# Row kurtosis on one core: 16 equal groups of 64 rows, loads in pieces, and an order written by hand

## The chip, the cores and the metric

The kernel runs on one core of a Trainium2 chip. The metric is the time of one execution in microseconds (us) on the device; lower is better. Engines are named as the profile names them: PE (matmul and transpose), DVE (vector), ACT (scalar activations), POOL (GpSimd) and SP (which issues loads). Each engine has its own queue of instructions and works it off in order; engines wait for one another through semaphores.

## The reference

The input `x` is 1024 rows of 8192 float32 values (33.55 MB). For each row the reference computes the excess kurtosis:

```python
mean = np.mean(x, axis=-1, keepdims=True)
std = np.std(x, axis=-1, keepdims=True)
z = (x - mean) / (std + 1e-8)
return (np.mean(z ** 4, axis=-1) - 3).astype(np.float32)
```

A kernel needs three sums for each row: the sum of the values, the sum of the squared differences from the mean, and the sum of their fourth powers. The result is N times the third divided by the square of the second, minus 3.

## The kernel before, in words

The rows are cut into 24 groups. `PLAN` gives a number k for each: a group has 128/k rows, and each row is spread over k partitions with 8192/k values in each. So k = 2 means 64 rows, a tile of 128 partitions by 4096 values, 2 MB. The plan begins with two groups of k = 8 and one of k = 4, has thirteen of k = 2, and ends with two of k = 4, two of k = 8 and four of k = 16. Each group is one load (L188, on SP's queue) into a slot of the `xpool`; there are 10 slots for the groups of k = 2.

For each group these steps follow:

- The mean. For k = 2 (the function `mean`, L116): PE transposes the 32 blocks of 128 columns and lets them add up in one PSUM tile `tps` (L123, "the turn" in what follows); DVE adds the two partitions of a row and writes the sum to both places, `red` (L129); PE multiplies `red` with a column of -1/8192, `negcol`, which gives minus the mean for each partition, `mps` (L134); ACT copies it to `nmu` (L137). For the other k (`mean_dve`, L92): DVE adds the halves of the tile with a running sum (L96), PE adds up the partitions of a row with the block matrix `blk[k]` (L103), ACT copies (L105).
- The square (L192): ACT writes (x - mean) squared over the tile and its row sums into a column of `sa`.
- The fourth power of the group before (`fourth`, L165): DVE multiplies the tile with itself and writes the sum into `sd` (L175). Each fifth group has it on ACT instead (L171), into a column of `sa`; the last group is halved between the two.
- When a batch of neighbouring groups with the same k is through, `finish_batch` (L145): PE adds the partitions of a row for the squares (`p2`, L151) and for the fourth powers (`p4`, L152 and L153), DVE forms the result (L155 to L160), and a DMA writes it out (L163). There are six batches.

The Python loop gives the order in which the work is stated. The order on each engine is then made by the framework's scheduler, which goes by its own model of durations, and semaphores are set by it too. POOL builds the block matrices (L52 to L57) for each k, clears `sa` and `sd` (L85, L86), and then makes the identity matrix `ident` (L109, L110) that the transposes need, and `negcol` (L114).

Of the kernel before, what the change touches and what calls it, by code (L numbers as in the profile page):

```python
# [7 lines left out]
f32 = mybir.dt.float32  # L8
bf16 = mybir.dt.bfloat16
AO = mybir.AluOpType  # L10
AF = mybir.ActivationFunctionType
P = 128


PLAN = [8, 8, 4, 2, 2, 2, 2, 2, 2, 2, 2, 2, 2, 2, 2, 2, 4, 4, 8, 8, 16, 16, 16, 16]
SLOTS = {2: 10, 4: 2, 8: 2, 16: 4}


@with_exitstack
def kernel(  # L20
    ctx: ExitStack,
    tc: tile.TileContext,
    x: bass.AP,
    out: bass.AP,
):
    nc = tc.nc
    n_rows, n_cols = x.shape
    neg_inv_n = -1.0 / float(n_cols)
    assert sum(P // k for k in PLAN) == n_rows

    xpool = ctx.enter_context(tc.tile_pool(name="xpool", bufs=1))
    const = ctx.enter_context(tc.tile_pool(name="const", bufs=1))
    junkp = ctx.enter_context(tc.tile_pool(name="junkp", bufs=1))
    small = ctx.enter_context(tc.tile_pool(name="small", bufs=6))
    fin = ctx.enter_context(tc.tile_pool(name="fin", bufs=2))
    psum = ctx.enter_context(tc.tile_pool(name="psum", bufs=2, space=bass.MemoryType.PSUM))
    psfin = ctx.enter_context(tc.tile_pool(name="psfin", bufs=1, space=bass.MemoryType.PSUM))


    warm = const.tile([P, 1], f32, name="warm")  # L40
    nc.vector.memset(warm, 0.0)
    nc.scalar.activation(out=warm, in_=warm, func=AF.Square)


    blk = {}

    def block_matrix(k):
        if k not in blk:
            r = P // k
            b = const.tile([P, P], f32, name=f"blk{k}")  # L50
            v = b.rearrange("p (r k) -> p r k", k=k)
            nc.gpsimd.memset(b, neg_inv_n)  # L52
            nc.gpsimd.affine_select(  # L53
                out=v, in_=v, pattern=[[-k, r], [0, k]], base=0,
                channel_multiplier=1, compare_op=AO.is_ge, fill=0.0,
            )
            nc.gpsimd.affine_select(  # L57
                out=v, in_=v, pattern=[[k, r], [0, k]], base=k - 1,
                channel_multiplier=-1, compare_op=AO.is_ge, fill=0.0,
            )  # L60
            blk[k] = b
        return blk[k]

    for k in PLAN:
        block_matrix(k)

    groups = []
    row = 0
    for k in PLAN:
        groups.append((row, k, P // k, n_cols // k))  # L70
        row += P // k


    batches = []
    for i, g in enumerate(groups):
        if batches and groups[batches[-1][0]][1] == g[1] and len(batches[-1]) < 64:
            batches[-1].append(i)
        else:
            batches.append([i])
    where = {}  # L80
    for b in batches:
        n = len(b)
        sa = const.tile([P, 2 * n], f32, name=f"sa{b[0]}")
        sd = const.tile([P, n], f32, name=f"sd{b[0]}")
        nc.gpsimd.memset(sa, 0.0)  # L85
        nc.gpsimd.memset(sd, 0.0)  # L86
        for j, i in enumerate(b):
            where[i] = (b, j, n, sa, sd)

    junk = junkp.tile([P, 1024], bf16, name="junk")  # L90

    def mean_dve(i, xt):  # L92
        row, k, r, w = groups[i]
        h = w // 2
        part = small.tile([P, 1], f32, name="part")
        nc.vector.tensor_tensor_reduce(  # L96
            out=junk[:, :h], in0=xt[:, :h], in1=xt[:, h:],
            scale=neg_inv_n if k == 1 else 1.0, scalar=0.0,
            op0=AO.add, op1=AO.add, accum_out=part)
        if k == 1:  # L100
            return part
        mps = psum.tile([P, 1], f32, name="mps")
        nc.tensor.matmul(mps, lhsT=blk[k], rhs=part, start=True, stop=True)  # L103
        nmu = small.tile([P, 1], f32, name="nmu")
        nc.scalar.copy(nmu, mps)  # L105
        return nmu

    ident = const.tile([P, P], f32, name="ident")
    nc.gpsimd.memset(ident, 1.0)  # L109
    nc.gpsimd.affine_select(  # L110
        out=ident, in_=ident, pattern=[[-1, P]], base=0,
        channel_multiplier=1, compare_op=AO.is_equal, fill=0.0)
    negcol = const.tile([P, 1], f32, name="negcol")
    nc.gpsimd.memset(negcol, neg_inv_n)  # L114

    def mean(i, xt):  # L116
        row, k, r, w = groups[i]
        if k > 2:
            return mean_dve(i, xt)
        ch = w // P  # L120
        tps = psum.tile([P, P], f32, name="tps")
        for c in range(ch):
            nc.tensor.matmul(tps, lhsT=xt[:, c * P:(c + 1) * P], rhs=ident,  # L123
                             start=c == 0, stop=c == ch - 1, is_transpose=True)
        red = small.tile([P, P], f32, name="red")
        if k == 1:
            nc.vector.tensor_copy(red, tps)
        else:
            nc.vector.tensor_reduce(  # L129
                out=red.rearrange("p (r k) -> p r k", k=k),  # L130
                in_=tps.rearrange("p (r k) -> p r k", k=k).unsqueeze(2).to_broadcast([P, r, k, k]),
                op=AO.add, axis=mybir.AxisListType.X)
        mps = psum.tile([P, 1], f32, name="mps")
        nc.tensor.matmul(mps, lhsT=red, rhs=negcol,  # L134
                         start=True, stop=True)
        nmu = small.tile([P, 1], f32, name="nmu")
        nc.scalar.copy(nmu, mps)  # L137
        return nmu

    def split(i, w):  # L140
        if i == len(groups) - 1:
            return w // 2
        return w if i % 5 == 2 else 0

    def finish_batch(b):  # L145
        _, _, n, sa, sd = where[b[0]]
        row, k, r, w = groups[b[0]]
        sel = blk[k].rearrange("p (r k) -> p r k", k=k)[:, :, 0]
        p2 = psfin.tile([n, r], f32, name="p2")
        p4 = psfin.tile([n, r], f32, name="p4")  # L150
        nc.tensor.matmul(p2, lhsT=sa[:, 0:n], rhs=sel, start=True, stop=True)  # L151
        nc.tensor.matmul(p4, lhsT=sa[:, n:2 * n], rhs=sel, start=True, stop=False)  # L152
        nc.tensor.matmul(p4, lhsT=sd, rhs=sel, start=False, stop=True)  # L153
        rec = fin.tile([n, r], f32, name="rec")
        nc.vector.reciprocal(rec, p2)  # L155
        kr = fin.tile([n, r], f32, name="kr")
        nc.vector.scalar_tensor_tensor(  # L157
            out=kr, in0=p4, scalar=-1.0, in1=rec, op0=AO.mult, op1=AO.mult)
        nc.vector.tensor_mul(kr, kr, rec)  # L159
        nc.vector.tensor_scalar_add(kr, kr, -3.0)  # L160
        dst = out[row:row + n * r].rearrange("(g r) -> g r", r=r)
        eng = nc.sync if b is batches[-1] else nc.scalar
        eng.dma_start(out=dst, in_=kr)  # L163

    def fourth(i):  # L165
        row, k, r, w = groups[i]
        b, j, n, sa, sd = where[i]
        xt = tiles[i]
        cl = split(i, w)
        if cl > 0:  # L170
            nc.scalar.activation(  # L171
                out=xt[:, :cl], in_=xt[:, :cl], func=AF.Square,
                accum_out=sa[:, n + j:n + j + 1])
        if cl < w:
            nc.vector.tensor_tensor_reduce(  # L175
                out=xt[:, cl:], in0=xt[:, cl:], in1=xt[:, cl:], scale=1.0, scalar=0.0,
                op0=AO.mult, op1=AO.add, accum_out=sd[:, j:j + 1])
        if j == n - 1:
            finish_batch(b)

    tiles = {}
    used = {}
    for i, (row, k, r, w) in enumerate(groups):
        s = used.get(w, 0)
        used[w] = s + 1
        xt = xpool.tile([P, w], f32, name=f"x{k}", tag=f"x{k}_{s % SLOTS[k]}")
        tiles[i] = xt
        nc.sync.dma_start(  # L188
            out=xt, in_=x[row:row + r, :].rearrange("r (k w) -> (r k) w", k=k))
        nmu = mean(i, xt)  # L190
        b, j, n, sa, sd = where[i]
        nc.scalar.activation(  # L192
            out=xt, in_=xt, func=AF.Square, bias=nmu, accum_out=sa[:, j:j + 1])
        if i > 0:
            fourth(i - 1)
    fourth(len(groups) - 1)


# [28 lines left out]
```

## Time and profile before

| | us |
|---|---|
| median of 3 runs | 134.70 |
| lowest and highest run | 134.06, 134.92 |
| the profiled execution | 134.22 |
| its span, first to last instruction | 132.5 |
| busy: ACT | 80.2 |
| busy: PE | 74.8 |
| busy: DVE | 73.6 |
| busy: POOL | 5.8 |

The mean granted clock of PE was 0.802. The loads moved 33.56 MB in 24 transfers. A profile line of a group of instructions reads: line, engine, operation, output <- input, shapes, count, busy time and mean duration, idle time of the engine just before, and what ended that idle time. In the slices, the span is cut into 40 equal parts of 3.3 us, and each digit is the busy share in tenths.

### The profile page before, as it was taken

The numbers are of one execution on the slowest core, as the hardware profiler recorded it, in microseconds if no ns is written. First come the engines' busy times: TensorE is split into PE (matmuls) and PEld (weight loads), VectorE is DVE, ScalarE is ACT, GpSimd is POOL, SyncE is SP. The second block draws the span as 40 slices with busy tenths as digits, with TensorE's granted clock in tenths as the row PEclk, the third lists the DMA queues.
The fourth block names the chain that finished last, engine by engine and source line by source line (L and its number), as shares of the span: only waits on it lengthen the run. The fifth ranks groups of instructions, "written<-read, shape, count | busy, mean of one in ns | idle before, by whom it ended". The sixth has DMA issues, their size and how long they took to land. (4 is left out here: it accounts for less than half of the span.)

```text
span 132.5 us, 1379 instructions
## 1 busy us (share of the span) xinstructions
PE 74.8 (56%) x500; PEld 69.0 (52%) x500; DVE 73.6 (56%) x98; ACT 80.2 (61%) x86; POOL 5.8 (4%) x31
## 2 busy tenths in 40 slices
PE   0223999419894298789403989168999202115430
PEld 0221989319794297779303979067989101014420
DVE  0458011580299709610996069931015999998881
ACT  4076608309292196999901948047899694449890
POOL 8900000000000000000000000000000000000000
PEclk9999999985699959999995599965589975555555
DMA  4999999999999999999999996000000000000000
GB/s 114 433 462 415 420 445 401 425 435 401 465 406 450 415 435 435 401 460 406 455 406 406 419 403 232 0 2 0 0 0 7 0 0 0 0 0 1 0 0 0
DMA packets 3511, 33.64 MB, mean 254 GB/s; under 512 B 433, under 2 KB 433, under 8 KB 1457
## 3 DMA queue, kind: packets, MB, share of 16 engines
q1 hardware_dynamic: 3464, 33.56, 60.5%
q8 instruction: 4, 0.07, 0.2%
q14 instruction: 3, 0.02, 0.0%
q10 hardware_dynamic: 40, 0.00, 0.0%
HBM read 33.55 MB, written 0.00 MB: 253 GB/s over the span
## 5 line engine op out<-in xcount | busy, mean ns | idle before, releaser
L175 DVE CUSTOM_DVE_ANT_0 x<-x 128x4096 f32<-128x4096 f32 (+4 forms) x19 | 57.4, 3027 | 10.1 <-ACT x L192 5.0
L192 ACT ACTIVATE x<-x,nmu 128x4096 f32<-128x4096 f32 (+3 forms) x24 | 61.7, 2573 | 1.3 <-DVE kr L160 0.6
L123 PE MATMUL tps<-ident,x 128*128 128x128 f32 x416 | 61.2, 318 | 0.3 <-DMA x<-in_x_dram 0.3
L123 PEld LDWEIGHTS tps<-ident,x 128*128 128x128 f32 x416 | 59.6, 172 | 0.4 <-issue 0.4
L129 DVE TENSOR_REDUCE red<-tps 128x128 f32<-128x256 f32 x13 | 5.5, 423 | 38.2 <-PE tps L123 38.2
L137 ACT COPY nmu<-mps 128x1 f32<-128x1 f32 x13 | 2.0, 155 | 36.0 <-PE mps L134 36.0
L134 PE MATMUL mps<-negcol,red 128*128 128x1 f32 x26 | 5.5, 282 | 27.4 <-DVE red L129 27.4
L134 PEld LDWEIGHTS mps<-negcol,red 128*128 128x128 f32 x26 | 4.7, 225 | 30.5 <-issue 19.1
L171 ACT ACTIVATE x<-x 128x2048 f32<-128x2048 f32 (+3 forms) x6 | 12.1, 2013 | 0.9 <-DVE rec L155 0.8
L103 PE MATMUL mps<-part,blk 128*128 128x1 f32 x22 | 6.1, 358 | 10.5 <-DVE part L96 10.5
L103 PEld LDWEIGHTS mps<-part,blk 128*128 128x128 f32 x22 | 5.4, 315 | 11.6 <-issue 7.7
L96 DVE CUSTOM_DVE_ANT_0 junk<-x 128x512 bf16<-128x512 f32 (+2 forms) x11 | 8.1, 737 | 5.7 <-DMA x<-in_x_dram 5.7
L105 ACT COPY nmu<-mps 128x1 f32<-128x1 f32 x11 | 1.4, 153 | 10.4 <-PE mps L103 10.4
L151 PE MATMUL p<-blk,sa 128*2 128x16 f32 (+4 forms) x12 | 1.6, 218 | 10.4 <-ACT x L192 8.7
L151 PEld LDWEIGHTS p<-blk,sa 128*2 128x2 f32 (+3 forms) x12 | 0.6, 85 | 11.0 <-ACT x L192 9.1
L153 PE MATMUL p<-blk,sd 128*2 128x16 f32 (+4 forms) x12 | 1.6, 222 | 5.4 <-DVE sd L175 5.3
L192 ACT ACTIVATION_READ_ACCUMULATOR x<-x,nmu 128x1 f32 x24 | 4.5, 187 | 0.0
L153 PEld LDWEIGHTS p<-blk,sd 128*2 128x2 f32 (+3 forms) x12 | 0.8, 92 | 5.7 <-DVE sd L175 4.0
L57 POOL TENSOR_SCALAR_AFFINE_SELECT blk<-blk 128x128 f32<-128x128 f32 x4 | 2.1, 545 | 0.0
L155 DVE RECIPROCAL rec<-p 2x16 f32<-2x16 f32 (+4 forms) x6 | 1.9, 317 | 0.3 <-PE p L151 0.2
L152 PE MATMUL p<-blk,sa 128*2 128x16 f32 (+4 forms) x12 | 1.5, 206 | 1.0 <-ACT x L171 0.8
L53 POOL TENSOR_SCALAR_AFFINE_SELECT blk<-blk 128x128 f32<-128x128 f32 x4 | 1.9, 501 | 0.0
(20 smaller groups left out, 11.5 us busy)
## 6 DMA issues: line engine op xcount, KB each, us to landing
x<-in_x_dram SPq DMA_DIRECT2D x13, 2048.0 KB, 27.9
x<-in_x_dram SPq DMA_DIRECT2D x3, 1024.0 KB
x<-in_x_dram SPq DMA_DIRECT2D x4, 512.0 KB, 3.9
x<-in_x_dram SPq DMA_DIRECT2D x4, 256.0 KB, 14.4
out_dram<-kr ACTq DMA_DIRECT2D x3, 0.1 KB
out_dram<-kr ACTq DMA_DIRECT2D x1, 3.2 KB
out_dram<-kr ACTq DMA_DIRECT2D x1, 0.2 KB
out_dram<-kr SPq DMA_DIRECT2D x1, 0.1 KB
```

The lines of the kernel that those rows point to most:

```text
L57: nc.gpsimd.affine_select(out=v, in_=v, pattern=[[k, r], [0, k]], base=k - 1, channel_multiplier=-1, compare_op=AO.is_ge, fill=0.0,)
L96: nc.vector.tensor_tensor_reduce(out=junk[:, :h], in0=xt[:, :h], in1=xt[:, h:], scale=neg_inv_n if k == 1 else 1.0, scalar=0.0, op0=AO.add ...
L103: nc.tensor.matmul(mps, lhsT=blk[k], rhs=part, start=True, stop=True)
L123: nc.tensor.matmul(tps, lhsT=xt[:, c * P:(c + 1) * P], rhs=ident, start=c == 0, stop=c == ch - 1, is_transpose=True)
L129: nc.vector.tensor_reduce(out=red.rearrange("p (r k) -> p r k", k=k), in_=tps.rearrange("p (r k) -> p r k", k=k).unsqueeze(2).to_broadcast ...
L134: nc.tensor.matmul(mps, lhsT=red, rhs=negcol, start=True, stop=True)
L137: nc.scalar.copy(nmu, mps)
L151: nc.tensor.matmul(p2, lhsT=sa[:, 0:n], rhs=sel, start=True, stop=True)
L153: nc.tensor.matmul(p4, lhsT=sd, rhs=sel, start=False, stop=True)
L171: nc.scalar.activation(out=xt[:, :cl], in_=xt[:, :cl], func=AF.Square, accum_out=sa[:, n + j:n + j + 1])
L175: nc.vector.tensor_tensor_reduce(out=xt[:, cl:], in0=xt[:, cl:], in1=xt[:, cl:], scale=1.0, scalar=0.0, op0=AO.mult, op1=AO.add, accum_out ...
L192: nc.scalar.activation(out=xt, in_=xt, func=AF.Square, bias=nmu, accum_out=sa[:, j:j + 1])
```

## The change

All 1024 rows go in 16 equal groups of 64 rows (k = 2), so that the mean is always taken by transposes; `mean_dve` and the block matrices are gone, and a matrix `sel` of 128 by 64 takes the place of the block matrices in the finish. Each group is loaded in four pieces of 1024 columns (512 KB each), and there are 12 slots of whole tiles. `tc.manual_schedule()` makes the order on each engine the order in which the program states it: all loads first on SP; on PE the turn, then the mean; on DVE the reduce of group i, then the fourth power of group i-1; on ACT the copy, the square, and then the fourth power of the first 512 columns of the same group. DVE takes the other 3584 columns. In the last group ACT takes 2304 columns and DVE 1792. The groups form three batches (12, 3 and 1); the finish is divided in `second_moment` and `finish`, and all outputs are issued on SP. `sa` and `sd` are no longer cleared, as all of their columns are written.

```diff
-PLAN = [8, 8, 4, 2, 2, 2, 2, 2, 2, 2, 2, 2, 2, 2, 2, 2, 4, 4, 8, 8, 16, 16, 16, 16]
-SLOTS = {2: 10, 4: 2, 8: 2, 16: 4}
+K = 2
+GROUPS = 16
+CHUNK = 1024
+SLOTS = 12
+ACT_S4 = 512
+LAST_ACT_S4 = 2304
+LAG_BATCH = 12
...
+    R = P // K
+    W = n_cols // K
+    xpool = ctx.enter_context(tc.tile_pool(name="xpool", bufs=SLOTS))
...
+    ctx.enter_context(tc.manual_schedule())
...
+    batches = [list(range(LAG_BATCH)), list(range(LAG_BATCH, GROUPS - 1)), [GROUPS - 1]]
...
+    def load(i):
+        xt = xpool.tile([P, W], f32, name="xt")
+        xts[i] = xt
+        src = x[i * R:(i + 1) * R, :].rearrange("r (k w) -> (r k) w", k=K)
+        for c in range(0, W, CHUNK):
+            nc.sync.dma_start(out=xt[:, c:c + CHUNK], in_=src[:, c:c + CHUNK])
+
+    def turn(i):
         tps = psum.tile([P, P], f32, name="tps")
+        tpss[i] = tps
+        for c in range(0, W, P):
+            nc.tensor.matmul(tps, lhsT=xts[i][:, c:c + P], rhs=ident,
+                             start=c == 0, stop=c == W - P, is_transpose=True)
+
+    def reduce(i):
         red = small.tile([P, P], f32, name="red")
+        nc.vector.tensor_reduce(
+            out=red.rearrange("p (r k) -> p r k", k=K),
+            in_=tpss[i].rearrange("p (r k) -> p r k", k=K).unsqueeze(2).to_broadcast([P, R, K, K]),
+            op=AO.add, axis=AX)
+
+    def mean(i):
         mps = psum.tile([P, 1], f32, name="mps")
+        nc.tensor.matmul(mps, lhsT=reds[i], rhs=negcol, start=True, stop=True)
         nmu = small.tile([P, 1], f32, name="nmu")
         nc.scalar.copy(nmu, mps)
+        mpss[i] = nmu
+
+    def square(i):
+        j, n, sa, sd = where[i]
+        nc.scalar.activation(out=xts[i], in_=xts[i], func=AF.Square, bias=mpss[i],
+                             accum_out=sa[:, j:j + 1])
+
+    def fourth_act(i, c):
+        j, n, sa, sd = where[i]
+        nc.scalar.activation(out=xts[i][:, :c], in_=xts[i][:, :c], func=AF.Square,
+                             accum_out=sa[:, n + j:n + j + 1])
+
+    def fourth_dve(i, c):
+        j, n, sa, sd = where[i]
+        nc.vector.tensor_tensor_reduce(
+            out=xts[i][:, c:], in0=xts[i][:, c:], in1=xts[i][:, c:], scale=1.0, scalar=0.0,
+            op0=AO.mult, op1=AO.add, accum_out=sd[:, j:j + 1])
+
+    def second_moment(b):
+        j, n, sa, sd = where[b[0]]
+        p2 = psfin.tile([n, R], f32, name="p2")
         nc.tensor.matmul(p2, lhsT=sa[:, 0:n], rhs=sel, start=True, stop=True)
+        rec = fin.tile([n, R], f32, name="rec")
+        nc.vector.reciprocal(rec, p2)
+        rec2 = fin.tile([n, R], f32, name="rec2")
+        nc.vector.scalar_tensor_tensor(
+            out=rec2, in0=rec, scalar=-1.0, in1=rec, op0=AO.mult, op1=AO.mult)
+        return rec2
+
+    def finish(b, rec2):
+        j, n, sa, sd = where[b[0]]
+        p4 = psfin.tile([n, R], f32, name="p4")
         nc.tensor.matmul(p4, lhsT=sa[:, n:2 * n], rhs=sel, start=True, stop=False)
         nc.tensor.matmul(p4, lhsT=sd, rhs=sel, start=False, stop=True)
+        kr = fin.tile([n, R], f32, name="kr")
+        nc.vector.tensor_mul(kr, p4, rec2)
         nc.vector.tensor_scalar_add(kr, kr, -3.0)
+        dst = out[b[0] * R:(b[0] + n) * R].rearrange("(g r) -> g r", r=R)
+        nc.sync.dma_start(out=dst, in_=kr)
+
+    L = GROUPS - 1
+    for i in range(GROUPS):
+        load(i)
+    for i in range(GROUPS):
+        turn(i)
+        reduce(i)
+        mean(i)
+        square(i)
+        if i >= 1:
+            fourth_dve(i - 1, ACT_S4)
+        if i < L:
+            fourth_act(i, ACT_S4)
+        if i == LAG_BATCH + 1:
+            finish(batches[0], second_moment(batches[0]))
+    rec2 = second_moment(batches[1])
+    rec2l = second_moment(batches[2])
+    fourth_act(L, LAST_ACT_S4)
+    fourth_dve(L, LAST_ACT_S4)
+    finish(batches[1], rec2)
+    finish(batches[2], rec2l)
```

The pools `psum` (two buffers each of `tps` and `mps`) and `psfin` (one buffer each of `p2` and `p4`) are as before.

More of the change, by code (lines that the diff above doesn't have):

```diff
@@ L42 @@
     nc.scalar.activation(out=warm, in_=warm, func=AF.Square)
[L45 to L106, printed above, removed]
     ident = const.tile([P, P], f32, name="ident")
@@ L114 @@
     nc.gpsimd.memset(negcol, neg_inv_n)
[L116 to L120, printed above, removed]
-        tps = psum.tile([P, P], f32, name="tps")
-        for c in range(ch):
-            nc.tensor.matmul(tps, lhsT=xt[:, c * P:(c + 1) * P], rhs=ident,
-                             start=c == 0, stop=c == ch - 1, is_transpose=True)
-        red = small.tile([P, P], f32, name="red")
[L126 to L132, printed above, removed]
+    sel = const.tile([P, R], f32, name="sel")
@@ new lines @@
+    nc.gpsimd.memset(sel, neg_inv_n)
+    nc.gpsimd.affine_select(
+        out=sel, in_=sel, pattern=[[-K, R]], base=0,
+        channel_multiplier=1, compare_op=AO.is_ge, fill=0.0)
+    nc.gpsimd.affine_select(
+        out=sel, in_=sel, pattern=[[K, R]], base=K - 1,
+        channel_multiplier=-1, compare_op=AO.is_ge, fill=0.0)
+    one = const.tile([1, 1], f32, name="one")
+    nc.gpsimd.memset(one, 1.0)
+    batches = [list(range(LAG_BATCH)), list(range(LAG_BATCH, GROUPS - 1)), [GROUPS - 1]]
@@ new lines @@
+    where = {}
+    for b in batches:
+        n = len(b)
+        sa = const.tile([P, 2 * n], f32, name=f"sa{b[0]}")
+        sd = const.tile([P, n], f32, name=f"sd{b[0]}")
+        for j, i in enumerate(b):
+            where[i] = (j, n, sa, sd)
+    xts = {}
+    tpss = {}
+    reds = {}
+    mpss = {}
+    def load(i):
[4 more added lines that the diff above has]
+            nc.sync.dma_start(out=xt[:, c:c + CHUNK], in_=src[:, c:c + CHUNK])
@@ L133, in mean @@
+    def mean(i):
         mps = psum.tile([P, 1], f32, name="mps")
-        nc.tensor.matmul(mps, lhsT=red, rhs=negcol,
-                         start=True, stop=True)
+        nc.tensor.matmul(mps, lhsT=reds[i], rhs=negcol, start=True, stop=True)
         nmu = small.tile([P, 1], f32, name="nmu")
         nc.scalar.copy(nmu, mps)
[L138 to L151, printed above, removed]
+        mpss[i] = nmu
@@ L152, in finish_batch @@
         nc.tensor.matmul(p4, lhsT=sa[:, n:2 * n], rhs=sel, start=True, stop=False)
         nc.tensor.matmul(p4, lhsT=sd, rhs=sel, start=False, stop=True)
[L154 to L195, printed above, removed]
@@ L196 @@
-    fourth(len(groups) - 1)
+        kr = fin.tile([n, R], f32, name="kr")
+        nc.vector.tensor_mul(kr, p4, rec2)
+        nc.vector.tensor_scalar_add(kr, kr, -3.0)
+        dst = out[b[0] * R:(b[0] + n) * R].rearrange("(g r) -> g r", r=R)
[14 more added lines that the diff above has]
+            finish(batches[0], second_moment(batches[0]))
```

10 lines of the change are left out of this document (5 added, 5 removed).

## The prediction

> **What bounds the kernel now.** I read the page first (engine totals, then the 40 slices), then the waits, then the timeline at two places.
>
> ```profile
> span 132.5 us, 1379 instructions
> PE 74.8 (56%) x500; PEld 69.0 (52%) x500; DVE 73.6 (56%) x98; ACT 80.2 (61%) x86; POOL 5.8 (4%) x31
> DVE  0458011580299709610996069931015999998881
> ACT  4076608309292196999901948047899694449890
> DMA  4999999999999999999999996000000000000000
> ```
>
> No engine is busy for more than 61% of the span. The DMA engines are full from slice 1 to slice 23 and stop in slice 24, at about 82 us; for the last 50 us no input moves, and DVE and ACT work off what is left. So the end is set by compute that fell behind the loads. Nor is that compute short of throughput: while the loads ran, DVE and ACT had many slices of 0 to 3. The waits say why.
>
> ```profile
> DVE red L129 <- PE tps L123: 38.2, 7, 6.3
> ACT nmu L137 <- PE mps L134: 36.0, 10, 6.0
> PE mps L134 <- DVE red L129: 27.4, 13, 7.5
> ```
>
> The columns are total us, times, longest. Three engines wait in a ring for one another. The timeline shows one turn of it, then a stretch where the order happens to be right:
>
> ```profile
> 24.56 4.43 DVE L175 CUSTOM_DVE_ANT_0 x<-x 128x4096 f32<-128x4096 f32 x1 [4.16 <-ACT x L192]
> 28.91 0.42 DVE L129 TENSOR_REDUCE red<-tps 128x128 f32<-128x256 f32 x1
> 29.38 0.59 PE L134 MATMUL mps<-negcol,red 128*128 128x1 f32 x2 [4.84 <-DVE red L129]
> 29.83 5.79 PE L123 MATMUL tps<-ident,x 128*128 128x128 f32 x26
> 35.66 0.42 DVE L129 TENSOR_REDUCE red<-tps 128x128 f32<-128x256 f32 x1 [6.33 <-PE tps L123]
> 36.81 3.74 ACT L192 ACTIVATE x<-x,nmu 128x4096 f32<-128x4096 f32 x1
> ...
> 50.95 0.16 ACT L137 COPY nmu<-mps 128x1 f32<-128x1 f32 x1 [0.98 <-PE mps L134]
> 51.14 3.72 ACT L192 ACTIVATE x<-x,nmu 128x4096 f32<-128x4096 f32 x1
> 54.98 3.63 ACT L171 ACTIVATE x<-x 128x4096 f32<-128x4096 f32 x1
> 55.45 3.69 PE L123 MATMUL tps<-ident,x 128*128 128x128 f32 x32
> 59.18 0.42 DVE L129 TENSOR_REDUCE red<-tps 128x128 f32<-128x256 f32 x1 [4.09 <-PE tps L123]
> 59.97 4.45 PE L123 MATMUL tps<-ident,x 128*128 128x128 f32 x39
> ```
>
> At 24.56 DVE takes a whole fourth power (4.43 us) ahead of the reduce that PE needs; PE stands for 4.84 us, then transposes at 5.79 us for 26 instead of 3.69 us for 32, since its clock has dropped to half:
>
> ```profile
> 30.00:31.00 1.00, 1.00 (x6) 1.00 (x6) 0.50 1.17 492
> 55.24 0.35 PE L134 MATMUL mps<-negcol,red 128*128 128x1 f32 x2 [0.77 <-DVE red L129]
> ```
>
> (The third column from the end is the granted clock.) A gap of 0.77 us does not cost the clock.
>
> **The change, group by group.** All 16 groups now have the form of the old 13 middle ones.
>
> *PE.* A turn of 32 transposes takes 3.69 us; from its end at 59.14 to the next turn's start at 59.97 are 0.8 us, with reduce and mean between them. Period 4.5 us, if DVE takes the reduce at once: the mean waits for it on PE, and the whole next turn is queued behind the mean.
>
> *ACT.* Copy to the end of the square is 50.95 to 54.98, 4.03 us; the added fourth power of 512 columns:
>
> ```profile
> L175 DVE CUSTOM_DVE_ANT_0 x<-x 128x4096 f32<-128x4096 f32 x11 | 48.6, 4422 | 9.3 <-ACT x L192 4.6 <-ACT nmu L137 4.6
> L175 DVE CUSTOM_DVE_ANT_0 x<-x 128x2048 f32<-128x2048 f32 x1 | 2.3, 2270 | 0.0
> L171 ACT ACTIVATE x<-x 128x2048 f32<-128x2048 f32 x2 | 3.8, 1910 | 0.8 <-DVE rec L155 0.8
> L171 ACT ACTIVATE x<-x 128x512 f32<-128x512 f32 x1 | 0.6, 613 | 0.0
> ```
>
> 0.61 us more: 4.64 us. *DVE.* From 4096 to 2048 columns is 1.05 ns a column, so 3584 columns are 3.88 us; with the reduce 4.3 us. The fourth power of group i-1 stands behind the reduce of group i, and its square ended about 5 us after its own turn, so DVE takes both back to back; where the ring now stalls DVE for 4 to 6 us a group, the next thing that is late is a piece of a load. All three are below what the loads allow.
>
> *Loads.* SP issues 64 instead of 24. Between 1 and 5 us it issued these:
>
> ```profile
> L188 SPq DMA_DIRECT2D x<-in_x_dram x7: 328/424/443, 0.8 to 4.3; - x7
> ```
>
> 0.33 to 0.44 us each (least, median, most), while a piece takes over 1.2 us to move, so SP keeps up; some seven are out before the first has landed, and seven pieces are 3.7 MB, nearly 9 us of queue. The added wait, for one of 12 slots, stands ahead of the last 16 pieces only: group 12 needs group 0's fourth powers, done near 20 us, and its turn to load comes near 50 us. I cost both at nothing; if the queue ran dry, it would be the rate that shows it. The rate remains. Rows get 4 KB instead of 16 KB, in pieces of 512 KB instead of 2 MB. The first two loads of before were 512 KB with 4 KB rows, the last eight were 512 and 256 KB with 4 and 2 KB rows:
>
> ```profile
> 4.29 0.83 DVE L96 CUSTOM_DVE_ANT_0 junk<-x 128x512 bf16<-128x512 f32 x1 [3.36 <-DMA x<-in_x_dram]
> 4.00:5.00 1.00, 0.00 (x0) 0.00 (x0) 0.71 (x1) 0.00 (x0) 1.00 (x3) 1.00 1.06 434
> 77.00:78.00 1.00, 0.39 (x5) 0.18 (x2) 0.63 (x2) 0.00 (x0) 0.00 (x0) 1.00 1.03 414
> 80.00:81.00 1.00, 1.00 (x11) 1.00 (x10) 1.00 (x1) 1.00 (x1) 0.00 (x0) 1.00 1.05 387
> ```
>
> The last column is GB/s. The bounds are 434 and 387; I take 420, between the 434 of the head and the 414 at 77 us, which are nearest in row length. A piece is then 1.25 us, and a group 4.99 us, above PE's 4.5 and ACT's 4.64: **the loads set the pace.** The first piece lands at 4.2 us, as now; the 64th at 4.2 + 63 x 1.25 = 82.8.
>
> Here the Trainium skill speaks against the change: "DMA: Bandwidth & Descriptors", section "Bandwidth", gives 341 GB/s for 1 MB and asks for transfers of at least 1 MiB. By 341 the stream would take 98 us and the sum would be about 115. The trace disagrees so far: 434 GB/s at 4 us, among 512 KB loads. The same page's table under "SWDGE vs HWDGE vs iDMA" has 408.7 GB/s for a load stream with 4 KiB rows; by that the sum would be 99 to 100.
>
> *Start.* PE begins cold, at 6.41 us for a turn:
>
> ```profile
> 13.03 6.41 PE L123 MATMUL tps<-ident,x 128*128 128x128 f32 x32 [0.27 <-DMA x<-in_x_dram]
> ```
>
> So turn 0 runs from 4.3 to 10.7, 2.5 us behind its loads; with 4.5 against 4.99 us PE has caught up by group 5 or 6, which hides the cold start. `ident` moves ahead of the masks on POOL (busy 5.8 us in all now) and so is ready before the first piece. The 11 half sums on DVE (L96) and the six small batches go: busy time at the start and in the last 20 us of before, not on the new path. The outputs of batch 0 move from ACT's queue to SP's, behind all 64 loads; nothing waits for them but the end, and they go out some 10 us ahead of it. The memsets of `sa` and `sd` on POOL go too; POOL is idle after 6.5 us now, so they gave nothing up. Batch 0's finish stands behind turn 13: three matmul pairs, some 0.8 us on PE ahead of turn 14, and four small operations, 1.1 us on DVE ahead of reduce 14. PE's slack of half a microsecond a group absorbs it in two groups, so I cost it at nothing; with that slack gone it is 1 us.
>
> *Tail.* When the last piece is down, 8 transposes remain (8/32 of 3.69, 0.92): turn 15 ends at T = 83.8. The steps after it:
>
> ```profile
> 106.34 3.71 ACT L192 ACTIVATE x<-x,nmu 128x4096 f32<-128x4096 f32 x1
> 110.19 0.39 PE L151 MATMUL p<-blk,sa 128*13 128x64 f32 x2 [4.08 <-ACT x L192]
> 115.42 0.54 DVE L155 RECIPROCAL rec<-p 13x64 f32<-13x64 f32 x1
> 130.22 0.16 DVE L160 TENSOR_SCALAR kr<-kr 4x8 f32<-4x8 f32 x1
> ```
>
> Turn end to square 1.2 (35.62 to 36.81); square to its second-moment matmul 3.85 (106.34 to 110.19); matmul 0.39, reciprocal 0.54, product 0.2 (an estimate from the 0.16 of the last row, at 64 columns instead of 8). DVE waits for the first and runs the other two ahead of `fourth_dve(15)`, which so starts at T + 6.2, with the handovers, and needs 1792 columns, 2.0 us plus the accumulator: T + 8.3. ACT's 2304 columns start at T + 5.0 and take 1.91 + 256 x 0.84 ns = 2.12, and so end a microsecond sooner. Then the earlier batch's product (its `p4` holds the only buffer) 0.25, the last `p4` matmuls 0.5, product and sum: the last DVE operation starts near T + 9.3. From such a start to the end of the span it is now 132.5 - 130.22 = 2.3. Tail 11.6; span 83.8 + 11.6 = 95.4.
>
> The profiled execution took 134.22 us with a span of 132.5, so 1.7 lie around it: **97.1, say 97.0 us**, against 134.22 (the median of the runs, 134.7, is 0.4% above).
>
> **Rivals.**
> 1. *The loads lose rate* to short rows and small pieces. For it: 387 GB/s at 80 us, all DMA engines full. Against: 434 at 4 us. (The rule of the Trainium skill quoted above is of this kind.) At 387 a piece is 1.355 us, the 64th lands 6.5 us later: 103.6. Chance 0.16.
> 2. *The pieces do nothing*: a turn waits for all four. Then 32 transposes follow the last landing, 3.69 instead of 0.92: 99.8. Against it:
>
> ```profile
> 128.54 0.20 PE L151 MATMUL p<-blk,sa 128*4 128x8 f32 x2 [1.75 <-ACT x L192]
> 129.01 0.40 ACT L171 ACTIVATE x<-x 128x256 f32<-128x256 f32 x1
> ```
>
> The matmul read its columns of `sa` while ACT had another column of that tile still to write, so waits go by part of a tile. Chance 0.07.
> 3. *PE becomes the bound*: gaps cost it the clock part of the time. With half of the groups cold (6.41 + 1.0, against 4.5), the mean period is 5.95: turn 0 ends at 10.7, so 10.7 + 15 x 5.95 + 11.6 + 1.7 = 113. Against it: gaps of 0.8 us kept 1.00 between 50 and 64 us. Chance 0.08.
> 4. *Slower than before*: the waits for pieces leave PE at 0.50 throughout. 4.3 + 16 x 6.41 + 15 x 1.0 (the cold gap, from the reduce at 28.91 to 29.83, and the handover) + 1.2 (batch 0, three times 0.39) + 11.6 + 1.7 = 136.4. It decides only if every stretch of about 5 us, with 4.2 us of PE work, counts as idle; the row at 55.24 speaks against it. Chance 0.03.
>
> **How the numbers follow.** Forecast, from 94.4 (434 GB/s: 63 pieces, 0.04 us less each) to 98.5: 0.66. With rivals 1 and 2 the range 94 to 104.5 holds 0.85 or somewhat more; rivals 3 and 4 stay out. One per cent, 1.3 us, is about what a measurement of this kernel can tell from no change. Faster by more: all cases but rival 4, 0.96; slower 0.03; within 1% 0.01, a mixture between rivals 3 and 4.
>
> **What would show it.** Right: reduces 4.9 to 5.0 us apart from group 6 on; DMA full until about 83 us; PE's transposes waiting for loads; clock 0.9 and up after the first 10 us; some 12 us from the last landing to the end. Wrong: ACT or DVE idle on PE for more than 1 us a group with the clock at 5 (rivals 3, 4), DMA full but below 400 GB/s (1), a first transpose of each group only after its fourth piece (2). The prediction fails altogether if a wait that I don't see ties turn i+1 to square i.

## The result, and the profile after

The changed kernel takes 102.16 us (median of 4 runs, 102.02 to 102.28), the kernel before 134.41 us beside it: a ratio of 0.760, 95% interval 0.757 to 0.763. The forecast was 97.0 us in a range of 94.0 to 104.5. The profiled execution took 102.13 us with a span of 100.4.

The page of the changed kernel, engine totals and slices (now 2.5 us each):

```profile
span 100.4 us, 1513 instructions
PE 73.0 (73%) x562; PEld 63.2 (63%) x562; DVE 69.2 (69%) x61; ACT 77.7 (77%) x82; POOL 1.3 (1%) x11
ACT  5000089999996798989797999898989897999910
PEclk9999999999999999999999999999999999999555
DMA  1999999999999999999999999999999999100000
GB/s 59 284 374 372 418 418 415 415 405 408 408 413 406 408 415 406 405 410 415 405 410 415 405 410 410 406 405 408 411 410 408 408 408 371 64 0 0 0 0 3
```

The engines are busy for about as long as before (DVE 73.6, ACT 80.2 then). What went is idle time: the last piece is in at 87.4 us, in slice 34, and only 13 us follow instead of 50. From the second group on PE keeps its full clock until the last three slices. The rate is 405 to 418 GB/s, and lower in the first four slices.

The waits of the changed kernel (total us, times, longest):

```profile
DVE red L100 <- PE tps L94: 26.4, 15, 10.9
PE mps L107 <- DVE red L100: 8.7, 14, 0.9
PE tps L94 <- DMA xt<-in_x_dram: 8.0, 14, 5.3
```

PE waited 27.4 us for the reduce, at worst 7.5; now 8.7 us, at worst 0.9, which is the reduce itself (0.42 us), the handovers and, at that one place, the finish of batch 0. The new row is PE waiting for pieces. One group in the timeline:

```profile
65.78 0.86 PEld L94 LDWEIGHTS tps<-ident,xt 128*128 128x128 f32 x8 [0.21 <-DMA xt<-in_x_dram]
67.06 1.09 PE L94 MATMUL tps<-ident,xt 128*128 128x128 f32 x8 [0.19 <-DMA xt<-in_x_dram]
68.19 0.42 DVE L100 TENSOR_REDUCE red<-tps 128x128 f32<-128x256 f32 x1 [0.89 <-PE tps L94]
68.54 3.88 DVE L124 CUSTOM_DVE_ANT_0 xt<-xt 128x3584 f32<-128x3584 f32 x1
73.31 0.42 DVE L100 TENSOR_REDUCE red<-tps 128x128 f32<-128x256 f32 x1 [0.89 <-PE tps L94]
```

Pieces land 1.28 us apart; after the last one PE has eight transposes left; reduces stand 5.12 us apart, and every engine has slack. The loads set the pace.

### The profile page after: what moved, and what is told of

The parts are those of the page before. It is cut to its first block, busy times and chain, and to the rows that moved or that the text cites. A ratio compares the mean times of both kernels' runs of the same rounds, so it can differ in the third digit from the quotient of the medians.

```text
span 100.4 us, 1513 instructions
## 1 busy us (share of the span) xinstructions
PE 73.0 (73%) x562; PEld 63.2 (63%) x562; DVE 69.2 (69%) x61; ACT 77.7 (77%) x82; POOL 1.3 (1%) x11
## 4 chain that ended last, share of the span: by engine, by line
DMA 77%; DVE 8%; ACT 8%; PE 1%; issue 1%; SPq 1%; ACTq 0%; DVEq 0%
DMA xt<-in_x_dram 77%; ACT xt L114 8%; DVE xt L124 6%; DVE rec L134 1%; SPq L88 1%; ACT xt L119 1%; DVE kr L146 1%; DVE red L100 0%; PE p L132 0%; PE p L143 0%; PE mps L107 0%; DVE rec L136 0%; DVE kr L147 0%; PE p L144 0%; ACTq L114 0%
## 5 line engine op out<-in xcount | busy, mean ns | idle before, releaser
L94 PE MATMUL tps<-ident,xt 128*128 128x128 f32 x512 | 67.1, 285 | 8.1 <-DMA xt<-in_x_dram 8.0
L94 PEld LDWEIGHTS tps<-ident,xt 128*128 128x128 f32 x512 | 59.3, 148 | 13.8 <-DMA xt<-in_x_dram 7.7
L124 DVE CUSTOM_DVE_ANT_0 xt<-xt 128x3584 f32<-128x3584 f32 (+1 forms) x16 | 60.3, 3766 | 0.2 <-ACT xt L114 0.2
L114 ACT ACTIVATE xt<-xt,nmu 128x4096 f32<-128x4096 f32 x16 | 59.5, 3718 | 0.9 <-ACT nmu L109 0.3
L119 ACT ACTIVATE xt<-xt 128x512 f32<-128x512 f32 (+1 forms) x16 | 11.6, 723 | 0.5
L132 PE MATMUL p<-sel,sa 128*12 128x64 f32 (+2 forms) x6 | 0.9, 244 | 3.9 <-ACT xt L114 3.9
L143 PE MATMUL p<-sel,sa 128*12 128x64 f32 (+2 forms) x6 | 1.1, 273 | 2.6 <-DVE kr L146 2.6
L119 ACT ACTIVATION_READ_ACCUMULATOR xt<-xt 128x1 f32 x16 | 3.0, 186 | 0.0
L114 ACT ACTIVATION_READ_ACCUMULATOR xt<-xt,nmu 128x1 f32 x16 | 2.9, 184 | 0.0
L134 DVE RECIPROCAL rec<-p 12x64 f32<-12x64 f32 (+2 forms) x3 | 1.6, 543 | 0.5 <-PE p L132 0.5
L124 DVE DVE_READ_ACCUMULATOR2_ANT sd<- 128x1 f32 x16 | 1.3, 82 | 0.0
```

Source lines behind the costliest of these rows:

```text
L94: nc.tensor.matmul(tps, lhsT=xts[i][:, c:c + P], rhs=ident, start=c == 0, stop=c == W - P, is_transpose=True)
L114: nc.scalar.activation(out=xts[i], in_=xts[i], func=AF.Square, bias=mpss[i], accum_out=sa[:, j:j + 1])
L119: nc.scalar.activation(out=xts[i][:, :c], in_=xts[i][:, :c], func=AF.Square, accum_out=sa[:, n + j:n + j + 1])
L124: nc.vector.tensor_tensor_reduce(out=xts[i][:, c:], in0=xts[i][:, c:], in1=xts[i][:, c:], scale=1.0, scalar=0.0, op0=AO.mult, op1=AO.add, ...
```

## The experiments

**The order on DVE alone.** Reduce and fourth power change places:

```diff
     for i in range(GROUPS):
         turn(i)
-        reduce(i)
-        mean(i)
-        square(i)
         if i >= 1:
             fourth_dve(i - 1, ACT_S4)
+        reduce(i)
+        mean(i)
+        square(i)
```

Expected: 

> One thing moved: on DVE the fourth power of group i-1 stands ahead of the reduce of group i instead of behind it. If the order on DVE is what frees the ring: the reduce waits for square i-1 (5.0 us after the reduce before) and for 3.9 us of fourth power, 8.9 us a group, last reduce near 146 us, 160 us in all, slower than before the change. If DVE's order is of no weight, since DVE is busy for 69% only: 102 to 104 us.

Measured: 158.83 us (two runs), ratio to the kernel before 1.183 (1.173 to 1.194). Its timeline:

```profile
60.82 3.89 DVE L124 CUSTOM_DVE_ANT_0 xt<-xt 128x3584 f32<-128x3584 f32 x1 [4.56 <-ACT xt L114]
64.64 0.42 DVE L100 TENSOR_REDUCE red<-tps 128x128 f32<-128x256 f32 x1
65.21 0.56 PE L107 MATMUL mps<-negcol,red 128*128 128x1 f32 x2 [4.89 <-DVE red L100]
65.62 5.03 PE L94 MATMUL tps<-ident,xt 128*128 128x128 f32 x32
69.83 3.89 DVE L124 CUSTOM_DVE_ANT_0 xt<-xt 128x3584 f32<-128x3584 f32 x1 [4.76 <-ACT xt L114]
```

9.0 us from one fourth power to the next: square, fourth power and reduce stand in one line. DVE waits 4.6 us for the square, PE 4.9 us for the reduce, and PE's gap costs it the clock: the granted clock falls to 0.50 from 65 to 68 us, and 32 transposes take 5.03 us instead of 3.69. The same work in another order of two instructions costs 57 us, and is slower than the kernel before.

**The order without the rest, and the rest without the order.** First, one line is added to the kernel before:

```diff
     psfin = ctx.enter_context(tc.tile_pool(name="psfin", bufs=1, space=bass.MemoryType.PSUM))
+    ctx.enter_context(tc.manual_schedule())
```

Expected: 

> The kernel before with one line added: every engine works in the order in which the program states the work (so on DVE the reduce of group i ahead of the fourth power of group i-1). Groups, whole loads, split of the fourth powers and finishes stay as they were. If the order is nearly the whole gain: the ring opens, the loads (4.90 us a group at 427 GB/s) or ACT (80 us busy) set the pace, 98 to 106 us. If the equal groups and the pieces are needed too: 110 to 130 us.

Measured: 127.58 us, ratio 0.951 (0.941 to 0.962). It lies in the second band: the order alone is not the gain. Its timeline (line numbers are one higher than before):

```profile
36.93 0.42 DVE L130 TENSOR_REDUCE red<-tps 128x128 f32<-128x256 f32 x1
41.61 0.42 DVE L130 TENSOR_REDUCE red<-tps 128x128 f32<-128x256 f32 x1
...
91.14 3.71 ACT L193 ACTIVATE x<-x,nmu 128x4096 f32<-128x4096 f32 x1
97.42 0.16 ACT L106 COPY nmu<-mps 128x1 f32<-128x1 f32 x1 [2.47 <-PE mps L104]
```

and the longest of its waits:

```profile
PE mps L104 <- DVE part L97: 24.4, 10, 7.9
```

In the middle the ring is open, 4.68 us a group. The time is lost in the small groups: their half sums (L97) stand on DVE behind fourth powers, PE waits 24.4 us for them, and the last eight groups, 4 MB, take from 97 us to the end at 125. The last square of the groups with k = 2 ends at 94.9 us (91.14 + 3.71), in the kernel before at 110.1 (106.34 + 3.71, a row that the prediction shows): 15.2 us sooner. From there to the end it is 30.2 us instead of 22.5.

The other way round, that line is taken out of the changed kernel:

```diff
-    ctx.enter_context(tc.manual_schedule())
```

Expected: 

> The changed kernel with that one line taken away: the framework's scheduler chooses the order on each engine. If the order is the gain: the ring is back, 115 us or more. If equal groups, pieces and the split of the fourth powers are the gain: 102 to 106 us.

Measured: 123.92 us (two runs), ratio 0.923 (0.911 to 0.934). Its timeline:

```profile
39.56 3.89 DVE L123 CUSTOM_DVE_ANT_0 xt<-xt 128x3584 f32<-128x3584 f32 x1 [0.74 <-ACT xt L113]
43.38 0.42 DVE L99 TENSOR_REDUCE red<-tps 128x128 f32<-128x256 f32 x1
43.94 0.56 PE L106 MATMUL mps<-negcol,red 128*128 128x1 f32 x2 [4.13 <-DVE red L99]
```

The ring is back: a fourth power ahead of the reduce, PE standing for 4.1 us (16.7 us in all for the reduce, 8.7 in the changed kernel). The loads ran as in the changed kernel and end before 88 us; what is late is the compute behind them. So the order alone gives 6.6 us and the rest alone 10.3, together 17; both at once give 32. Half of the gain exists only when the two meet: without the order the equal groups run into the ring, and without the equal groups the order loses in the small ones about half of what it gains ahead of them.

**What the shape of the loads costs.** Two edits of one constant:

```diff
-CHUNK = 1024
+CHUNK = 4096   (and 2048)
```

Expected for 4096: 

> Each group is loaded in one transfer of 2 MB with rows of 16 KB; the order stays. If the loads set the pace and short rows cost rate: 4.90 us a group instead of 5.12 (8 rows of 611 ns on each DMA engine), the first group lands near 7.9 us, the last near 81.4, then a whole turn of 3.7 us and the tail of 11.9: 98.8 us. If the rate has nothing to do with the shape of the loads: 5.12 us a group, 102 us. If PE or ACT set the pace: no change or slower by the later start, 104 us.

Expected for 2048: 

> Two transfers of 1 MB for each group, rows of 8 KB. If row length sets the rate: 4.96 us a group, the last half lands near 82.6 us, 16 transposes are left: 98 us. If the rate has nothing to do with the shape: 100.4 us.

Measured: 100.84 us (ratio 0.751, interval 0.747 to 0.756) with whole loads, 99.81 us (0.744, 0.739 to 0.749) with halves. Both are below the changed kernel, and 2.0 and 1.8 us above what I expected. PE in the kernel with whole loads:

```profile
8.72 5.59 PE L94 MATMUL tps<-ident,xt 128*128 128x128 f32 x32 [8.72 <-DMA xt<-in_x_dram]
29.67 3.69 PE L94 MATMUL tps<-ident,xt 128*128 128x128 f32 x32 [0.92 <-DMA xt<-in_x_dram]
...
83.60 3.69 PE L94 MATMUL tps<-ident,xt 128*128 128x128 f32 x32
```

The first load is 0.8 us later than assumed. The fifth is used at 29.67 us, 20.95 us after the first, where four loads of 4.9 us take 19.6: another 1.35 us are lost once, and the last turn starts at 83.60 us instead of 81.4. By the trace's record of landings the last load was in at 83.3 us, so the finish of batch 0, which here delays reduce 14, costs at most 0.3 us at the end. With halves the same step is 0.7 us, and the last half comes 0.5 us late once more. The last section says what goes with these steps.

The last piece of the kernel with halves:

```profile
84.46 1.97 PE L94 MATMUL tps<-ident,xt 128*128 128x128 f32 x16 [0.31 <-DMA xt<-in_x_dram]
```

It starts at 84.46 us, the last piece of the changed kernel at 87.40, though it is twice as large. To separate row length, size of a transfer, stride and computation, two kernels load and do nothing else, six stages of five groups each (one profiled execution of each).

Expected: 

> Leaves out all computation (the output is zeros): thirty groups of 2 MB are loaded in six stages of five groups. Stages: one transfer with 16 KB rows; four of 512 KB with 4 KB rows, strided in memory; four of 512 KB with 4 KB rows, contiguous in memory; one of 2 MB with 4 KB rows; four of 512 KB with 16 KB rows on 32 partitions each; two of 1 MB with 8 KB rows. If the row length sets the rate, in GB/s: 427, 410, 410, 410, 425, 423. If the size of a transfer does: 427, 410, 410, 427, 410, 418. If the stride in memory does: 427, 410, 427, 410, 427, 418. If the computation beside them does: 427 in all.

Expected: 

> Leaves out all computation (the output is zeros): six stages of five groups, 10.5 MB each: four transfers of 512 KB with 4 KB rows, contiguous in memory; two of 1 MB with 16 KB rows on 64 partitions each; one of 2 MB with 4 KB rows; eight of 256 KB with 2 KB rows; four of 512 KB with 4 KB rows, strided; one of 2 MB with 16 KB rows. Start: if a strided source makes the start slow, the stretch from 3 to 4 us moves 420 to 430 GB/s here as in the kernel before, against 213 in the changed kernel; if not, about 213. Rates: if both the row and the transfer cost time, 409, (64 partitions) 210 or 425, 416, 380, 409, 427 GB/s; if only the row does, the first, third and fifth are alike.

The windows of the first, in the middle of each stage (last column GB/s; stages in the order of the expectation):

```profile
10.00:25.00 15.00, 0.00 (x0) 0.00 (x0) 1.00 1.01 434
35.00:50.00 15.00, 0.00 (x0) 0.00 (x0) 1.00 1.03 409
58.00:73.00 15.00, 0.00 (x0) 0.00 (x0) 1.00 1.03 411
88.00:103.00 15.00, 0.00 (x0) 0.00 (x0) 1.00 1.03 416
110.00:145.00 35.00, 0.00 (x0) 0.00 (x0) 1.00 1.00 211
157.00:175.00 18.00, 0.00 (x0) 0.00 (x0) 1.00 1.01 421
```

and of the second:

```profile
3.00:4.00 1.00, 0.00 (x0) 0.00 (x0) 1.00 1.00 402
4.00:5.00 1.00, 0.00 (x0) 0.00 (x0) 1.00 0.87 340
10.00:25.00 15.00, 0.00 (x0) 0.00 (x0) 1.00 1.03 414
30.00:50.00 20.00, 0.00 (x0) 0.00 (x0) 1.00 1.00 211
85.00:100.00 15.00, 0.00 (x0) 0.00 (x0) 1.00 1.03 416
110.00:125.00 15.00, 0.00 (x0) 0.00 (x0) 1.00 1.06 387
135.00:150.00 15.00, 0.00 (x0) 0.00 (x0) 1.00 1.03 409
160.00:175.00 15.00, 0.00 (x0) 0.00 (x0) 1.00 1.01 431
```

Strided 4 KB rows in 512 KB transfers move 409 GB/s with nothing beside them, the same as in the changed kernel: neither the computation nor its order matters. Contiguous rows move 411 and 414 in these windows. The times at which the loads landed are finer than a window: strided and contiguous pieces both land 1.28 us apart (410 GB/s), so the stride has no weight once the stream runs. Groups with 4 KB rows in one transfer of 2 MB land 5.04 us apart (416), groups with 16 KB rows 4.90 us apart (428, where the windows read 431 to 434). Most of the loss is thus the row; 416 against 410 is left to the four transfers in place of one. Rows of 2 KB fall to 387, the rate that bounded the prediction. The start stays open: contiguous rows began with 402 GB/s from 3 to 4 us where the changed kernel had 213, but fell to 340 in the next microsecond. The kernel with whole loads, whose first load is one stretch of 2 MB in memory, had 279 there, so the stride alone is not the reason.

**Is anything else on the path?** ACT's share is cut, and the slots:

```diff
-ACT_S4 = 512
+ACT_S4 = 64
```
```diff
-SLOTS = 12
+SLOTS = 5
```

Expected: 

> ACT takes 64 columns of each fourth power instead of 512, so DVE takes 4032: DVE 4.8 us a group instead of 4.3, ACT 4.2 instead of 4.7. If the loads set the pace at 5.12 us: within 1% of 102.2 us, some tenths more for the longer last fourth powers on DVE. If DVE's share were on the path: 16 times 0.47, 109 us.

Expected: 

> 5 slots instead of 12. A slot is free 10.6 us after its group has landed, and the queue holds 9 us of pieces, so a fifth group (20.5 us later) is issued in time: 102.2 us. If the wait for slots were on the path: 104 us or more.

Measured: 102.78 us (ratio 0.765, 0.759 to 0.771) and 102.03 us (0.763, 0.759 to 0.768); the changed kernel has 0.760. DVE's work grew by 0.47 us in each of 15 groups, and the time by 0.6 in all. The split is needed only so far that DVE stays below the loads; 12 slots are not needed.

**A version that beats both.** Pieces only where they are waited for, and the last reciprocal behind the last fourth power:

```diff
-        for c in range(0, W, CHUNK):
+        step = CHUNK if i >= GROUPS - 2 else 2 * CHUNK if i == 0 or i >= GROUPS - 4 else W
+        for c in range(0, W, step):
...
-    rec2 = second_moment(batches[1])
-    rec2l = second_moment(batches[2])
+    finish(batches[1], second_moment(batches[1]))
     fourth_act(L, LAST_ACT_S4)
     fourth_dve(L, LAST_ACT_S4)
-    finish(batches[1], rec2)
-    finish(batches[2], rec2l)
+    finish(batches[2], second_moment(batches[2]))
```

with `LAG_BATCH = 9`. Expected: 

> Pieces only where they are waited for: group 0 in halves, groups 1 to 11 whole, 12 and 13 in halves, 14 and 15 in quarters; batch 0 ends with group 8; and in the tail the last reciprocal stands behind the last fourth power on DVE, which so starts 1.2 us sooner. If rows and transfers set the rate: 4.9 us a group in the middle, the last piece lands near 83.5 us (87.4 in the changed kernel), and the tail is 11 us: 97 us. If the rate is that of the changed kernel whatever the shape: 101 us.

Measured: 98.84 us, ratio 0.736 (0.730 to 0.742). Its last reduces:

```profile
81.12 0.42 DVE L101 TENSOR_REDUCE red<-tps 128x128 f32<-128x256 f32 x1
85.69 0.42 DVE L101 TENSOR_REDUCE red<-tps 128x128 f32<-128x256 f32 x1
```

4.6 us apart, and neither PE nor ACT stands for a load between them: at the end these two set the pace, still making up for the whole loads. So in a second version the whole loads end with group 6 (`i >= 7` in place of `i >= GROUPS - 4`), and ACT takes 320 columns instead of 512.

Expected: 

> The kernel with mixed pieces once more: group 0 in halves, 1 to 6 whole, 7 to 13 in halves, 14 and 15 in quarters, and ACT takes 320 columns of each fourth power instead of 512. If PE and ACT (4.5 and 4.64 us a group) had not made up by group 15 what the whole loads cost them (3.7 us from a landing to the end of its turn instead of 1): now they have, the last turn ends within 1.5 us of the last landing near 83 us, 97.4 us. If the last landing itself is late: no change, 98.8 us.

Measured: 98.14 us, ratio 0.734 (0.731 to 0.737), the fastest kernel here:

```profile
84.31 1.09 PE L95 MATMUL tps<-ident,xt 128*128 128x128 f32 x8 [0.15 <-DMA xt<-in_x_dram]
85.44 0.42 DVE L101 TENSOR_REDUCE red<-tps 128x128 f32<-128x256 f32 x1 [0.58 <-PE tps L95]
94.17 0.18 DVE L148 TENSOR_SCALAR kr<-kr 1x64 f32<-1x64 f32 x1
```

The last turn now ends 1.1 us after its last piece, as expected; that piece came at 84.3 instead of 83, 1.0 us of it through the same one-off step as above. From the last reduce to the last DVE operation are 8.7 us, in the changed kernel 9.4: the moved reciprocal is worth 0.6 us, half of the 1.2 expected, since the finish of batch 1 keeps DVE until 91.1 us.

## Why the prediction was right, and where it was off

The mechanism was right: the order opened the ring, the loads took over as the bound, and the three engines kept below them. The reversed order on DVE came out at 158.8 us where its expectation, worked out by the same steps, gave 160. The clock stayed full, which is against rivals 3 and 4, and PE took pieces as they landed, which is against rival 2.

What was off is one term of the sum and its start: 102.1 us against 97.1. That lies above the forecast's own 94.4 to 98.5 and inside the range through the room left for rivals 1 and 2. It comes near rival 1's 103.6 partly by luck: the rate makes up 1.9 us of the miss, and the rest are terms that no rival had. Rows of the changed kernel's timeline:

```profile
5.26 6.56 PE L94 MATMUL tps<-ident,xt 128*128 128x128 f32 x32 [5.26 <-DMA xt<-in_x_dram]
24.90 1.09 PE L94 MATMUL tps<-ident,xt 128*128 128x128 f32 x8 [0.18 <-DMA xt<-in_x_dram]
27.47 2.15 PE L94 MATMUL tps<-ident,xt 128*128 128x128 f32 x16 [0.51 <-DMA xt<-in_x_dram]
28.52 0.86 PEld L94 LDWEIGHTS tps<-ident,xt 128*128 128x128 f32 x8 [0.22 <-DMA xt<-in_x_dram]
87.40 0.86 PEld L94 LDWEIGHTS tps<-ident,xt 128*128 128x128 f32 x8 [0.24 <-DMA xt<-in_x_dram]
88.53 0.42 DVE L100 TENSOR_REDUCE red<-tps 128x128 f32<-128x256 f32 x1 [0.50 <-PE tps L94]
93.57 0.37 PE L132 MATMUL p<-sel,sa 128*1 128x64 f32 x2 [3.91 <-ACT xt L114]
94.71 2.03 DVE L124 CUSTOM_DVE_ANT_0 xt<-xt 128x1792 f32<-128x1792 f32 x1
97.89 0.18 DVE L147 TENSOR_SCALAR kr<-kr 1x64 f32<-1x64 f32 x1
```

- **The rate of the loads**, the mis-sized term. 63 pieces after the first took 82.1 us (5.26 to 87.40), 1.30 us each; I had 1.25. In the steady part it is 1.28 us (409 to 410 GB/s), so 1.9 us of the miss (63 x 0.03) are the rate of 4 KB rows. I took 420 as a value between 434 and 414. Both are the rate of a single microsecond, and the view books a packet where it begins: from 7 to 8 us it reads 533 for the kernel before. In the microsecond with 434, 9 of the 97 packets also had 8 KB rows already. The trace of before had a better figure: its 4 KB packets took 159 ns each (median), as they do in the changed kernel (160), and 8 of them on each of 16 engines make 1.27 to 1.28 us a piece. (Of the last eight loads, which the prediction gives 4 and 2 KB rows, the first two had 8 KB rows; the row at 77 us is of the two with 4 KB.) The Trainium skill's 408.7 GB/s for 4 KiB rows ("DMA: Bandwidth & Descriptors", under "SWDGE vs HWDGE vs iDMA") agrees with the 409 here. Its 341 GB/s for 1 MB, which the page gives for loads issued from GpSimd, is not what a full queue from SP does here: halves of 1 MB moved 421.
- **The first piece** landed at 5.2 us instead of 4.2, and the stream stayed slow to about 10 us (372 and 374 GB/s in slices 2 and 3): 1.0 and some 0.5 us. I had taken the first landing of before; why the stream starts more slowly here stays open.
- **One slip**: the pieces used at 24.90 and 27.47 us are 2.6 us apart, and the one after came at 28.52, 3.6 us after the first where two pieces take 2.6. So 1.1 us stayed lost, though the rate did not dip (405 to 413 GB/s in slices 8 to 11). See the last section.
- **The tail** was 11.9 us for 11.6. Step by step from the turn's end T = 88.50: the second-moment matmul at T + 5.07 (expected 5.05), DVE's last fourth power at T + 6.21 (6.2), the last DVE operation at T + 9.39 (9.3), and 2.5 us from there to the end (2.3). From the last landing to T were 1.1 us, for 1.0. Together these terms are 4.9 of the 5.0 us.
- **Batch 0** was absorbed, as costed: reduce 14 came 5.40 us after reduce 13, reduce 15 only 4.71 us after that, on its piece. With whole loads, where the slack is smaller, it cost at most 0.3 us.
- The cold first turn took 6.56 us (6.41). The page's 9s for the clock there are no measurement: the trace's clock entries begin at 11.2 us, and in the kernel with halves, where they begin at 9.0 us, PE goes from 6 to 11 transposes a microsecond at that point. PE had caught up by group 3, not 5 or 6, because the loads were slower. The slots and the split cost nothing, as costed.

## What to carry to other kernels

When no engine is busy for two thirds of the span and three of them wait for one another in turn, read the order on the engine that serves two of them: here a 0.42 us reduce put behind a 3.9 us fourth power costs 57 us. The order and the shape of the work belong together: each alone gave a fifth to a third of what both gave. Cut loads into pieces only where something waits for the piece (the first and the last groups), and take the rate of a stream from a long stretch, or from the time of one packet, with the same row length.

## What the runs showed of the hardware

- A load onto 32 or onto 64 partitions at a time ran at 211 GB/s, half of the 410 to 428 of 2 MB and 512 KB loads onto 128 with 4 and 16 KB rows (by their landings), though several were queued. I had expected 410 to 427 for the 32, and 210 or 425 for the 64. The Trainium skill ("SBUF — State Buffer", section "Door 1: The DMA port swizzle") puts 32 and 64 partitions at the same bandwidth, which agrees.
- The slip coincides with a fetch of instructions. The DMA queues of the changed kernel:

```profile
q8 instruction: 4, 0.07, 0.3%
```

Four packets of 16 KB took 0.3% of 16 engines' span, 1.2 us each (0.003 x 16 x 100.4 / 4; by the trace 1.03 to 1.11), where a row of 16 KB takes 0.6 (4.9 us for the 8 rows of one engine in a 2 MB load). One of them began at 25.2 us, between the two pieces where the 1.1 us were lost. Each load leaves 16 completion marks in the trace, as many as there are DMA engines. Up to the piece that landed at 24.86 us the last mark came 0.30 us behind the fifteenth; from the next piece on, at 27.34, it came 1.1 to 1.2 us behind, while the other 15 kept their step. So one share of every piece fell behind by about one such packet and never caught up; a piece has landed only when its slowest share is in, and no bytes are lost to the rest. The second packet delayed the landings by another 0.16 us, the last two by nothing. Such a step, 0.7 to 1.5 us, stands at the first of these packets in all eleven kernels here that compute, the kernel before among them. The two kernels that only load have no such packets and no such step within a stage. What is not tried is a kernel that computes without the fetch.
